# The causal triangle in PSUM behind each unit's maximum, and the forget gates' logarithm on other engines

## The chip, the cores and the metric

The kernel runs on one core of a Trainium2 chip. The metric is the device time of one execution in microseconds (us), as the median of several runs. Beside the runs there is one execution taken with the hardware profiler; its rows give the start and the duration of every instruction on every engine. TensorE (PE) multiplies matrices, and its weight loads (PEld) overlap with its matmuls. VectorE (DVE), ScalarE (ACT) and GpSimd (POOL) do the elementwise work, and SyncE (SP) issues most of the transfers. SBUF is the large on-chip memory; PSUM is the small one into which PE writes, in banks of 512 fp32 numbers per partition. PE, ACT and DVE touch PSUM in this kernel, POOL does not.

## The reference

One layer over 1024 tokens of width 1024. The input is normalised, scaled and shifted, and projected at once to the queries, keys, values and gates of two groups of eight heads of width 64, and to eight forget gates. Cut to what the change touches:

```python
log_f = log_sigmoid(ff + b_f)                    # (seq, 8 heads)
f_cum = cumsum(log_f, axis=seq)

# forgetting attention (FoX), for a block of 128 queries against all keys so far
s = q @ k.T * scale
s = s + (f_q[:, None] - f_k[None, :])
s = where(k_pos <= q_pos, s, -inf)               # the causal triangle
p = softmax(s)
out = p @ v

# stick-breaking attention, in the other eight heads
z = q @ k.T * scale
log_keep = where(k_pos < q_pos, log_sigmoid(-z), 0)
w = where(k_pos < q_pos, exp(log_sigmoid(z) + sum of the later log_keep), 0)
out = w @ v
```

The head outputs are multiplied by SiLU gates, projected, multiplied by a gate, added to the residual and normalised again. Since the softmax is taken over keys, the term `f_q` of a query drops out of it; the kernel only uses `-f_cum` of the keys.

## The kernel before, in words

All matrix products are taken with each operand split into a high and a low fp32r part, so that one product costs three matmuls (`L256` to `L258` for the projections `m`, `L311` to `L313` for the values, `L833` to `L835` for the output).

Attention is cut into 128 **units** (p, h, i): pair of heads p (0 to 3 are stick-breaking, 4 to 7 are FoX), head h in the pair, block of 128 queries i. A unit has 128 x (i+1)*128 scores `S` (`L411`, `L412`), all of them in one PSUM tile of two banks. A stick-breaking unit then runs two sigmoids on ACT (`kp` `L430`, `be` `L431`), a running product on DVE (`L436`, `L440`) that reads a tile `floor` in PSUM, and a multiplication on POOL (`L442`). A FoX unit runs, on DVE, one custom instruction that adds the forget row `fb` to the scores and takes the maximum (`a`, `nm`, `L418`), on ACT the exponential with its sum `l` (`L423`), on DVE the reciprocal of `l` (`L424`), and on POOL the scaling (`L425`). Two units later PE transposes the weights (`T`, `L459`), ACT and DVE copy them out as high part (`pt`, `L461`) and low part (`L462`), and after every second unit PE multiplies them with the values into a tile `pv` (`L474`): 4 to 16 matmuls, first those of the high parts, then those of the low parts. ACT and DVE evacuate `pv` (`L493`, `L494`).

**The forget gates.** The raw gates `fsb` come out of the value product of group 1 (`L323`). `forget_logs` makes log-sigmoid of them as min(x,0) - ln(1+exp(-|x|)): |x| on DVE (`L343`), exponential and logarithm on ACT (`L344`, `L345`), the rest on DVE (`L346`), and a scan over the blocks of 128 tokens on DVE (`L349`). Twelve steps later `forget_rows` sums over the tokens with two matmuls into `fcum` (`L360`, `L361`), copies the negative out on ACT (`L363`), transposes it on PE (`frow`, `L366`) and stores it to `f_dr` in HBM, from where `load_fb` reads a row of 1024 numbers for each head, on 128 partitions at once (`L375`, on ACT's queue).

**The triangle.** `att_causal` (`L396`) adds a 128 x 128 triangle of zeros and -1e30 to the diagonal block of `fb`, on DVE, before the unit that needs it. For i running downwards, the block that was masked for one unit is never read again by the later ones of that head.

**Order.** PE's order is written out by hand: for each unit the scores, a share of projection work from a list of fillers, `pv` of finished pairs, transposes, more fillers. The order of SP, DVE, ACT and POOL is that of a planner that simulates a timeline while the program is built and puts each instruction on its engine where it expects its inputs to be ready; `after(...)` pins an instruction behind another. Each engine runs its list strictly in that order.

**PSUM.** Eight banks: two for `acc`, two for `T`, two for `S`, one called `pv` and one called `fl`. In the first half `fl` holds `floor`; in the second half `pv_tile` alternates between `pv` and `fl`.

## Time and profile before

| | |
|---|---|
| median of 3 runs | 699.13 us (698.71 to 699.32) |
| profiled execution, its own time | 699.99 us |
| its span, first to last instruction | 698.2 us |
| granted clock of TensorE | 0.996 |
| PE busy | 676.0 us, 97% of the span |
| DVE, ACT, POOL busy | 483.7, 385.0, 410.6 us |
| stick-breaking units | about 93 to 357 us |
| FoX units | about 355 to 626 us |
| last matmul ends | 690.05 us |

A row of the timeline has: start, duration, engine, line and operation, output<-inputs, shapes, how many instructions were merged, and in square brackets the idle time of the engine before it with what ended it. A row of a list of waits has: who waited for whom, the microseconds in total, how often, and the longest. PE is busy nearly all the time, so what another engine does costs time only where PE stands and waits.

### The profile page before, as it was taken

Reading aid. Unit: us, or ns where it says so; the run is one execution under the profiler, and the core shown is the slowest. Engines: PE = TensorE matmul, PEld = TensorE weight load, DVE = VectorE, ACT = ScalarE, POOL = GpSimd, SP = SyncE. Lnnn points to the kernel's source line nnn. Section 1 sums busy time; section 2 is a strip of 40 time slices with the busy share of each in tenths; the row PEclk is TensorE's granted clock in tenths of the full one; section 3 lists DMA queues with packets and bytes.
Section 4 is the critical chain, followed back from the end, with each engine's and each line's share of the span. In section 5 each row is a group of like instructions: output and inputs, shape, how many; then the busy total and the mean of one; then the engine's idle time right before and its main releaser. Section 6 shows DMA issues by size and latency. Waiting matters only on the chain.

```text
span 698.2 us, 11781 instructions
## 1 busy us (share of the span) xinstructions
PE 676.0 (97%) x4033; PEld 589.0 (84%) x4033; DVE 483.7 (69%) x931; ACT 385.0 (55%) x866; POOL 410.6 (59%) x530
## 2 busy tenths in 40 slices
PE   7999989999999999999999999999999999999995
PEld 4789887888997888889988877889988889888884
DVE  5985678767657676767686684758576767784644
ACT  5667567856658576666664554645564666531000
POOL 4560487656437566556388897868483464665412
PEclk9999999999999999999999999999999999999998
DMA  8953451112102122112144554345241299143301
GB/s 313 415 215 128 113 176 53 28 39 49 42 9 69 40 53 55 38 46 61 29 134 145 174 164 155 112 116 164 95 143 51 58 283 364 56 162 113 119 31 60
DMA packets 44027, 81.59 MB, mean 117 GB/s; under 512 B 5120, under 2 KB 18880, under 8 KB 43072
## 3 DMA queue, kind: packets, MB, share of 16 engines
q1 hardware_dynamic: 42816, 76.65, 33.5%
q10 hardware_dynamic: 1152, 4.19, 2.0%
q8 instruction: 32, 0.52, 0.3%
q14 instruction: 27, 0.22, 0.1%
HBM read 60.34 MB, written 16.29 MB: 110 GB/s over the span
## 4 chain that ended last, share of the span: by engine, by line
PE 76%; DVE 7%; DMA 5%; POOL 4%; ACT 4%; issue 3%; SPq 0%; POOLq 0%; DVEq 0%; ACTq 0%
PE pv L474 9%; PE m L256 8%; PE m L257 8%; PE m L258 8%; PE T L459 8%; PE o L835 4%; PE o L833 4%; PE o L834 4%; PE S L412 4%; PE S L411 4%; PE v L311 3%; PE v L313 3%; PE v L312 3%; DMA wss<-in_w_ss_dram 1%; DMA raw<-in_w_qkg_dram 1%
## 5 line engine op out<-in xcount | busy, mean ns | idle before, releaser
L256 PE MATMUL m<-uh,whi 128*128 128x512 f32 x304 | 126.3, 415 | 0.5 <-DVE kl L244 0.5
L257 PE MATMUL m<-ul,whi 128*128 128x512 f32 x304 | 119.8, 394 | 0.0
L258 PE MATMUL m<-uh,wlo 128*128 128x512 f32 x304 | 119.6, 394 | 0.0
L462 DVE TENSOR_TENSOR pt<-T,pt 128x512 fp32r<-128x512 f32 (+2 forms) x192 | 100.6, 550 | 16.1 <-ACT pt L461 14.9
L442 POOL TENSOR_TENSOR be<-be,kp 128x127 f32<-128x127 f32 (+3 forms) x64 | 77.1, 1205 | 34.9 <-DVE kp L440 25.9
L461 ACT CAST pt<-T 128x512 fp32r<-128x512 f32 (+2 forms) x192 | 85.7, 480 | 17.2 <-PE T L459 13.6
L436 DVE TENSOR_TENSOR_SCAN kp<-kp,floor 128x512 f32<-128x512 f32 (+2 forms) x64 | 65.2, 1018 | 32.4 <-ACT kp L430 31.4
L474 PE MATMUL pv<-pt,v 128*128 128x256 f32 (+3 forms) x640 | 81.7, 272 | 3.8 <-DVE pt L462 3.8
L474 PEld LDWEIGHTS pv<-pt,v 128*128 128x128 f32 (+1 forms) x640 | 77.4, 163 | 9.0 <-DVE pt L462 4.7
L425 POOL TENSOR_SCALAR a<-a,l 128x1024 f32<-128x1024 f32 (+3 forms) x64 | 48.3, 755 | 43.8 <-DVE l L424 31.2
L423 ACT ACTIVATE a<-a,nm 128x1024 f32<-128x1024 f32 (+3 forms) x64 | 49.8, 778 | 40.5 <-DVE nm L418 40.1
L258 PEld LDWEIGHTS m<-uh,wlo 128*128 128x128 f32 x304 | 57.1, 188 | 13.5
L411 PE MATMUL S<-k,q 128*128 128x512 f32 (+5 forms) x192 | 66.6, 348 | 1.5 <-ACT be L431 0.8
L412 PE MATMUL S<-kl,qz 128*128 128x512 f32 (+5 forms) x192 | 65.5, 342 | 0.0
L256 PEld LDWEIGHTS m<-uh,whi 128*128 128x128 f32 x304 | 57.3, 188 | 9.2 <-DVE kl L244 0.9
L257 PEld LDWEIGHTS m<-ul,whi 128*128 128x128 f32 x304 | 57.4, 189 | 8.0
L495 POOL TENSOR_TENSOR ty<-ty,sg 64x256 f32<-64x256 f32 x64 | 47.7, 745 | 26.5 <-DVE ty L494 12.5
L418 DVE CUSTOM_DVE_ANT_0 a<-S,fb 128x1024 f32<-128x1024 f32 (+3 forms) x64 | 48.2, 754 | 15.9 <-PE S L412 7.8
L430 ACT ACTIVATE kp<-S 128x128 f32<-128x128 f32 (+3 forms) x64 | 41.7, 651 | 31.9 <-PE S L412 28.6
L311 PE MATMUL v<-whi_v,uh 128*128 128x256 f32 (+1 forms) x192 | 56.0, 292 | 0.7 <-DVE kl L244 0.7
L389 ACT CAST qz<-q 64x128 fp32r<-64x128 f32 x128 | 37.4, 295 | 31.3 <-PE S L412 30.0
L313 PE MATMUL v<-wlo_v,uh 128*128 128x256 f32 (+1 forms) x192 | 54.2, 282 | 0.0
(284 smaller groups left out, 1628.6 us busy)
## 6 DMA issues: line engine op xcount, KB each, us to landing
raw<-in_w_qkg_dram SPq DMA_DIRECT2D x38, 256.0 KB, 3.0
wss<-in_w_ss_dram SPq DMA_DIRECT2D x7, 1024.0 KB, 9.0
x<-in_x_dram SPq DMA_DIRECT2D x8, 512.0 KB, 7.1
k<-k SPq DMA_DIRECT2D x32, 128.0 KB, 2.3
wg<-in_w_gate_dram SPq DMA_DIRECT2D x8, 512.0 KB, 5.0
raw_o<-in_w_out_dram SPq DMA_DIRECT2D x16, 256.0 KB, 2.7
fb<-f_dr ACTq DMA_DIRECT2D x8, 512.0 KB, 4.3
wo_dr<-whi_o SPq DMA_DIRECT2D x16, 256.0 KB, 2.4
```

What stands on the lines that cost most here:

```text
L256: nc.tensor.matmul(acc, hi[:, c], u_hi[kt][:, s], start=(kt == 0), stop=False)
L257: nc.tensor.matmul(acc, hi[:, c], u_lo[kt][:, s], start=False, stop=False)
L258: nc.tensor.matmul(acc, lo[:, c], u_hi[kt][:, s], start=False, stop=(kt == NB - 1))
L311: nc.tensor.matmul(acc[:, :n], u_hi[kt][:, ts_], hi[:, s], start=(kt == 0), stop=False)
L313: nc.tensor.matmul(acc[:, :n], u_hi[kt][:, ts_], lo[:, s], start=False, stop=(kt == NB - 1))
L411: nc.tensor.matmul(S[:, s, :w], qst[p][h][:, qs], kst[p][h][:, ks], start=True, stop=False)
L412: nc.tensor.matmul(S[:, s, :w], z, klo[p][:, ks], start=False, stop=True)
L436: nc.vector.tensor_tensor_scan(rv, rv, floor[0][:, 512 - n:][:, ::-1], initial=0.0, op0=ALU.mult, op1=ALU.max)
L442: nc.gpsimd.tensor_tensor(be[:, :ke - 1], be[:, :ke - 1], kp[:, 1:ke], op=ALU.mult)
L461: nc.scalar.copy(hi[:, :n, qo:qo + P], t3)
L462: nc.vector.tensor_tensor(lo[:, :n, qo:qo + P], t3, hi.bitcast(F32)[:, :n, qo:qo + P], op=ALU.subtract)
L474: nc.tensor.matmul(acc[:m, q0:256], vt[p][:, kb, h * P:h * P + m], pt[:, kb % 4, q0:], start=start, stop=stop)
```

## The change

Three things change.

1. **Log-sigmoid** is made as min(x,0) + ln(sigmoid(|x|)): |x|, sigmoid and logarithm on ACT, the minimum and the sum on POOL. The scan over blocks leaves this step.
2. **The sums of the gates.** Two matmuls write to two parts of one PSUM tile: the totals of all blocks (ones x `flf`, 65 columns) and the sums within a block. The scan over blocks runs on DVE from PSUM, in `forget_rows`; DVE instead of ACT then combines and negates the two.
3. **The triangle** is copied once to PSUM by ACT (`ps_causal`), into the bank `fl`, after the last stick-breaking unit's scores are issued. `pv_tile` no longer alternates: all of `pv` goes through one bank. Each add of the triangle is pinned behind the maximum of the preceding unit; the very first one, which still reads the triangle from SBUF, is pinned behind the last running product of the stick-breaking units.

```diff
     def forget_logs():
         ff = fsb.rearrange("p h t -> p (h t)")
         ab = cp.tile([P, 64], F32, tag="fab", name="fab")
         lf = flf[:, 1:]
-        nc.vector.scalar_tensor_tensor(ab, ff, -1.0, ff, op0=ALU.mult, op1=ALU.max)
-        nc.scalar.activation(ab, ab, AF.Exp, scale=-1.0)
-        nc.scalar.activation(ab, ab, AF.Ln, bias=1.0)
-        nc.vector.scalar_tensor_tensor(lf, ff, 0.0, ab, op0=ALU.min, op1=ALU.subtract)
-        pre = ff
-        nc.vector.tensor_tensor_scan(pre, flf[:, 0:64], later.rearrange("p h t -> p (h t)"), initial=0.0,
-                                     op0=ALU.add, op1=ALU.mult)
-        return lf, pre
+        nc.scalar.activation(ab, ff, AF.Abs)
+        nc.scalar.activation(ab, ab, AF.Sigmoid)
+        nc.scalar.activation(ab, ab, AF.Ln)
+        nc.gpsimd.tensor_scalar(ff, ff, 0.0, 1.0, op0=ALU.min, op1=ALU.mult)
+        nc.gpsimd.tensor_tensor(lf, ff, ab, op=ALU.add)
+        return lf
 ...
-        fp = t_tile("fcum")[:, :64]
-        nc.tensor.matmul(fp, tri, lf, start=True, stop=False)
-        nc.tensor.matmul(fp, ones.to_broadcast([P, P]), pre, start=False, stop=True)
+        fp = t_tile("fcum")
+        nc.tensor.matmul(fp[:, 64:129], ones.to_broadcast([P, P]), flf, start=True, stop=True)
+        nc.tensor.matmul(fp[:, :64], tri, lf, start=True, stop=True)
+        pre = fsb.rearrange("p h t -> p (h t)")
+        nc.vector.tensor_tensor_scan(pre, fp[:, 64:128], later.rearrange("p h t -> p (h t)"), initial=0.0,
+                                     op0=ALU.add, op1=ALU.mult)
         fc = cp.tile([P, 64], F32, tag="fab", name="fc")
-        nc.scalar.activation(fc, fp, AF.Copy, scale=-1.0)
+        nc.vector.scalar_tensor_tensor(fc, fp[:, :64], -1.0, pre, op0=ALU.mult, op1=ALU.subtract)
 ...
-            nc.vector.tensor_tensor(f[:, dg], f[:, dg], causal, op=ALU.add)
+            nc.vector.tensor_tensor(f[:, dg], f[:, dg], ps_causal[0][:, :P] if ps_causal else causal, op=ALU.add)
 ...
-            nc.vector.tensor_tensor_reduce(out=v3(a), in0=S[:, :ns, :w], in1=v3(f),
+            rows = nc.vector.tensor_tensor_reduce(out=v3(a), in0=S[:, :ns, :w], in1=v3(f),
                                            op0=ALU.add, op1=ALU.min, scale=-1.0, scalar=BIG,
                                            accum_out=nm)
             if following:
-                att_causal(following)
+                with after(rows):
+                    att_causal(following)
 ...
+            with after(scan):                      # scan: the unit's last running product
+                att_causal(following)
 ...
-        acc = pv_tile(f"pv_{p}_{h}_{j}", p >= 4 and j % 2 == 1)
+        acc = pv_tile(f"pv_{p}_{h}_{j}")
 ...
             if k == 16 * 4 - 1:
                 load_fb(0)
                 load_fb(1)
-                att_causal(units[k + 1])
 ...
+            if k == 16 * 4 - 1:
+                ps_causal.append(ps.tile([P, 512], F32, tag="fl", bufs=1, name="ps_causal"))
+                nc.scalar.copy(ps_causal[0][:, :P], causal)
```

What this does to the engines' lists is seen in two places. The orders of PE and SP stay as they were, but for the two matmuls of `fcum` changing places; the lines up to 342 keep their numbers, later ones move by up to five.

First, DVE's list around the forget gates (`fsb` are the gates, `kp_1_1_7` and `kp_2_0_0` the running products of two successive units, `pt1` the low parts of transposed weights, `T` the transposes). Before:

```order
L462 TENSOR_TENSOR pt1_1_1_2_1_2443<-T_1_1_4_1_2444,pt0_1_1_2_1_2442 128x128
L343 SCALAR_TENSOR_TENSOR fab_2460<-fsb_129 128x64
L436 SCALAR_TENSOR_TENSOR kp_1_1_7_2471<-kp_1_1_7_2471,floor_863 128x512
L440 SCALAR_TENSOR_TENSOR kp_1_1_7_2471<-kp_1_1_7_2471,floor_863 128x512
L346 SCALAR_TENSOR_TENSOR flf_130<-fsb_129,fab_2460 128x64
L349 SCALAR_TENSOR_TENSOR fsb_129<-flf_130,later_132 128x64
L462 TENSOR_TENSOR pt1_1_1_2_0_2434<-T_1_1_5_0_2494,pt0_1_1_2_0_2433 128x4x128
L462 TENSOR_TENSOR pt1_1_1_2_1_2443<-T_1_1_5_1_2501,pt0_1_1_2_1_2442 128x2x128
```

After the change:

```order
L465 TENSOR_TENSOR pt1_1_1_2_1_2443<-T_1_1_4_1_2444,pt0_1_1_2_1_2442 128x128
L437 SCALAR_TENSOR_TENSOR kp_1_1_7_2471<-kp_1_1_7_2471,floor_863 128x512
L441 SCALAR_TENSOR_TENSOR kp_1_1_7_2471<-kp_1_1_7_2471,floor_863 128x512
L465 TENSOR_TENSOR pt1_1_1_2_0_2434<-T_1_1_5_0_2494,pt0_1_1_2_0_2433 128x4x128
L465 TENSOR_TENSOR pt1_1_1_2_1_2443<-T_1_1_5_1_2501,pt0_1_1_2_1_2442 128x2x128
```

Three instructions have left the stretch, and the low parts of unit (1,1,5) now follow the running product directly. The scan and the negation stand further down the list, behind the running product of unit (2,0,4).

Second, DVE's list where FoX goes over from one pair of heads to the next (`fb_2` and `fb_3` are the forget rows of the two heads of pair 5, `fb_1` that of the second head of pair 4, `a` and `nm` the weights and the maximum of a unit; unit (5,0,7) with `fb_2` follows unit (4,1,0)). Before:

```order
L418 ISA a_4_1_0_5038,nm_4_1_0_5039<-S_4_1_0_5035,fb_1_4121 128x128
L418 ISA nm_4_1_0_5039 128x1
L424 RECIPROCAL l_4_1_0_5040<-l_4_1_0_5040 128x1
L396 TENSOR_TENSOR fb_3_5047<-fb_3_5047,causal_71 128x128
L250 SCALAR_TENSOR_TENSOR sg_5_4885<-sg_5_4885,m_5_2_0_4995 128x512
L462 TENSOR_TENSOR pt1_4_1_1_0_5021<-T_4_1_2_0_5072,pt0_4_1_1_0_5020 128x3x128
L418 ISA a_5_0_7_5095,nm_5_0_7_5096<-S_5_0_7_5090,fb_2_4620 128x1024
```

After the change:

```order
L418 ISA a_4_1_0_5041,nm_4_1_0_5042<-S_4_1_0_5038,fb_1_4122 128x128
L418 ISA nm_4_1_0_5042 128x1
L396 TENSOR_TENSOR fb_2_4623<-fb_2_4623,ps_causal_4138 128x128
L425 RECIPROCAL l_4_1_0_5043<-l_4_1_0_5043 128x1
L250 SCALAR_TENSOR_TENSOR sg_5_4888<-sg_5_4888,m_5_2_0_4998 128x512
L465 TENSOR_TENSOR pt1_4_1_1_0_5024<-T_4_1_2_0_5075,pt0_4_1_1_0_5023 128x3x128
L418 ISA a_5_0_7_5098,nm_5_0_7_5099<-S_5_0_7_5093,fb_2_4623 128x1024
```

The first add to `fb_3`, which only unit (5,1,7) needs, stood eight units ahead of that one, right behind the unit after which the load of `fb_3` is issued. Now the place holds the add to `fb_2` for the very next unit, with the triangle from PSUM; `fb_2` was loaded eight units earlier. The first adds to `fb_2` and to `fb_4` to `fb_7` move in the same way.

More of the change, by code (lines that the diff above doesn't have):

```diff
@@ L342, in forget_logs, with forget_rows @@
         lf = flf[:, 1:]
-        nc.vector.scalar_tensor_tensor(ab, ff, -1.0, ff, op0=ALU.mult, op1=ALU.max)
-        nc.scalar.activation(ab, ab, AF.Exp, scale=-1.0)
-        nc.scalar.activation(ab, ab, AF.Ln, bias=1.0)
-        nc.vector.scalar_tensor_tensor(lf, ff, 0.0, ab, op0=ALU.min, op1=ALU.subtract)
-        pre = ff
-        nc.vector.tensor_tensor_scan(pre, flf[:, 0:64], later.rearrange("p h t -> p (h t)"), initial=0.0,
-                                     op0=ALU.add, op1=ALU.mult)
-        return lf, pre
-    def forget_rows(lf, pre):
+        nc.scalar.activation(ab, ff, AF.Abs)
[4 more added lines that the diff above has]
+        return lf
+    def forget_rows(lf):
         scratch = att_tile("fscratch")
@@ L378, in tile_hybrid_layer @@
     st_w, st_pt = {}, {}
-    floor = []
+    floor, ps_causal = [], []
     zq = {}
@@ L435, in att_scores @@
             rv = kp[:, ke - n:ke][:, ::-1]
-            nc.vector.tensor_tensor_scan(rv, rv, floor[0][:, 512 - n:][:, ::-1], initial=0.0,
-                                         op0=ALU.mult, op1=ALU.max)
+            scan = nc.vector.tensor_tensor_scan(rv, rv, floor[0][:, 512 - n:][:, ::-1], initial=0.0,
+                                                op0=ALU.mult, op1=ALU.max)
             if ke > n:
                 rv = kp[:, :ke - n][:, ::-1]
-                nc.vector.tensor_tensor_scan(rv, rv, floor[0][:, 0:1].to_broadcast([P, ke - n]),
-                                             initial=kp[:, ke - n:ke - n + 1], op0=ALU.mult, op1=ALU.max)
+                scan = nc.vector.tensor_tensor_scan(rv, rv, floor[0][:, 0:1].to_broadcast([P, ke - n]),
+                                                    initial=kp[:, ke - n:ke - n + 1], op0=ALU.mult, op1=ALU.max)
+            with after(scan):
+                att_causal(following)
             nc.gpsimd.tensor_tensor(be[:, :ke - 1], be[:, :ke - 1], kp[:, 1:ke], op=ALU.mult)
@@ L774, in gen_forget @@
             yield
-        yield from forget_rows(*logs)
+        yield from forget_rows(logs)
     wo = {}
```

## The prediction

> **What bounds the kernel now.** The page's busy times and the list of waits of TensorE come first, since a change elsewhere can only win back what TensorE stands still (columns of a wait: total us, times, longest):
>
> ```profile
> PE 676.0 (97%) x4033; PEld 589.0 (84%) x4033; DVE 483.7 (69%) x931; ACT 385.0 (55%) x866; POOL 410.6 (59%) x530
> ...
> PE pv L474 <- DVE pt L462: 3.8, 5, 1.6
> PE sc_all L163 <- DVE sc L160: 3.3, 1, 3.3
> ...
> 690.09 0.42 DVE L848 SCALAR_TENSOR_TENSOR r<-xr,o 128x256 f32<-128x256 f32 x1 [1.94 <-PE o L835]
> ```
>
> The span is 698.2 us, so PE is idle for 22.2 us of it. 3.3 of them come before the first matmul, and 8.1 behind the last one, whose result DVE takes at 690.09; the change touches neither. So some 11 us are left to be won between, and nearly half of them are in these rows of PE's timeline:
>
> ```profile
> 220.85 0.98 PE L474 MATMUL pv<-pt,v 128*64 128x256 f32 x7 [1.64 <-DVE pt L462]
> 410.19 1.06 PE L459 MATMUL T<-ident,a 128*128 128x128 f32 x7 [0.24 <-DVE pt L462]
> 411.44 0.50 PE L411 MATMUL S<-k,q 128*128 128x512 f32 x1 [0.19 <-DVE nm L418]
> 414.79 1.22 PE L474 MATMUL pv<-pt,v 128*64 128x256 f32 x9 [0.41 <-DVE pt L462]
> 433.69 0.75 PE L474 MATMUL pv<-pt,v 128*64 128x256 f32 x5 [1.21 <-DVE pt L462]
> 469.00 0.74 PE L474 MATMUL pv<-pt,v 128*64 128x256 f32 x5 [0.15 <-DVE pt L462]
> 541.98 0.44 PE L411 MATMUL S<-k,q 128*128 128x384 f32 x1 [0.50 <-DVE nm L418]
> ```
>
> All of them wait for DVE. The reader is to see that each has a cause in what the change edits. A further point is how to size them: a matmul of 512 columns is shown with 0.40 us, yet the next one starts 0.23 us later.
>
> ```profile
> 217.82 0.40 PE L256 MATMUL m<-uh,whi 128*128 128x512 f32 x1
> 218.05 0.40 PE L257 MATMUL m<-ul,whi 128*128 128x512 f32 x1
> ```
>
> So a matmul's shown end lies some 0.16 us behind the moment at which the next could have followed, and every stop of PE is 0.16 us longer than its bracket.
>
> **The forget gates' logarithm.** DVE, ACT and POOL around 217 us, before the change:
>
> ```profile
> 214.54 1.28 ACT L344 ACT_TABLE_LOAD   x1
> 215.83 0.26 ACT L344 ACTIVATE fab<-fab 128x64 f32<-128x64 f32 x1
> 216.11 1.28 ACT L345 ACT_TABLE_LOAD   x1
> 217.57 0.84 ACT L461 CAST pt<-T 128x512 fp32r<-128x512 f32 x2
> 218.43 1.28 ACT L430 ACT_TABLE_LOAD   x1
> ...
> 217.69 1.23 DVE L346 SCALAR_TENSOR_TENSOR flf<-fsb,fab 128x64 f32<-128x64 f32 x1 [0.94 <-ACT fab L345]
> 218.95 1.26 DVE L349 TENSOR_TENSOR_SCAN fsb<-flf,later 128x64 f32<-128x64 f32 x1
> 220.13 0.99 DVE L462 TENSOR_TENSOR pt<-T,pt 128x512 fp32r<-128x512 f32 x2
> ...
> 218.79 2.51 POOL L126 TENSOR_TENSOR wlo<-raw,whi 128x512 fp32r<-128x512 f32 x2
> ```
>
> DVE waits 0.94 us for the logarithm, and two instructions of 64 elements then take 2.5 us, while POOL runs back to back. The low parts that PE wants (`L462`) start only at 220.13. The change takes these DVE instructions away and, by the order, puts the low parts right behind the running product. On ACT the sigmoid needs no load of its own, as the stick-breaking units use it; the order has one load fewer in this place. ACT's part is then |x|, sigmoid, load, logarithm: 214.5 + 0.26 + 0.26 + 1.28 + 0.26 = 216.6 (0.26 as in the `fab` row, for each of the three), so the high parts follow at 216.6 instead of 217.57, and the low parts end near 216.6 + 0.6 + 1.1 = 218.3. PE wants them at 220.85 - 1.64 = 219.2. The stop goes: 1.64 + 0.16 = 1.80 us, with 0.9 us to spare.
>
> [...]
>
> The two instructions on POOL come to its list between `L125`, `L442` and `L126`. Nothing of that size is in the trace: each lies between nothing and half of the 2.51 us that two `L126` of eight times the elements take. Fixed costs apart, an eighth of 1.25 is 0.16, so I take 0.3. POOL is then 0.6 us later at 221, where the product `be` of the next unit waits for it; its transposes come two units later. Nothing on PE, then.
>
> **The sums.** The scan and the negation now stand between the matmuls of `fcum` and the transpose `frow`, on DVE:
>
> ```profile
> 236.92 0.39 PE L361 MATMUL fcum<-fsb,ones 128*128 128x64 f32 x2
> 237.63 0.48 DVE L440 TENSOR_TENSOR_SCAN kp<-kp,floor 128x128 f32<-128x128 f32 x1
> 239.34 0.27 PE L366 MATMUL frow<-ident,fc 128*64 128x128 f32 x1
> ```
>
> By the order they follow `L440`, which ends at 238.11. A scan of 128 elements takes 0.48 here, so 64 take at most that; with 0.3 us for each of the two (my estimate, from that scan), `fc` is ready near 238.7, 0.6 us ahead of the transpose. Nothing, then; if the scan takes the 1.26 us of the old `L349`, `fc` is ready at 239.7 and PE stops for some 0.5 us. I take 0 and keep both ends for the range. The evacuation `L494` that they push back by 0.6 us has no reader before the next `pv`.
>
> **The triangle.** Its group, one of DVE's whose reading side is PSUM, and what DVE waits for there:
>
> ```profile
> L396 DVE TENSOR_TENSOR fb<-fb,causal 128x128 f32<-128x128 f32 x64 | 39.1, 612 | 12.7 <-DMA fb<-f_dr 11.5
> L320 DVE TENSOR_TENSOR v<-v,v 128x128 fp32r<-128x128 f32 x34 | 9.6, 282 | 6.2 <-ACT v L319 5.8
> ```
>
> The same shape takes 612 ns on the mean with both inputs in SBUF and 282 with one in PSUM. So 64 x 0.33 = 21 us of DVE's time go, and with them 11.5 us of standing for the transfer of `fb`. What counts is where PE was stopped by it:
>
> ```profile
> 404.77 4.15 DVE L396 TENSOR_TENSOR fb<-fb,causal 128x128 f32<-128x128 f32 x1
> 431.70 0.87 DVE L396 TENSOR_TENSOR fb<-fb,causal 128x128 f32<-128x128 f32 x1 [3.75 <-DMA fb<-f_dr]
> 467.03 0.85 DVE L396 TENSOR_TENSOR fb<-fb,causal 128x128 f32<-128x128 f32 x1 [2.78 <-DMA fb<-f_dr]
> 535.47 0.90 DVE L396 TENSOR_TENSOR fb<-fb,causal 128x128 f32<-128x128 f32 x1 [1.15 <-DMA fb<-f_dr]
> ...
> 407.49 1.29 POOL L126 TENSOR_TENSOR wlo_o<-raw_o,whi_o 128x512 fp32r<-128x512 f32 x1
> 408.75 0.66 POOL L125 TENSOR_SCALAR whi_o<-raw_o 128x512 fp32r<-128x512 f32 x1
> ```
>
> At 404.77 the add lasts until POOL, busy without a gap, goes from one instruction to the next at 408.75; the stops of 0.24 and 0.19 follow. At 431.70, 467.03 and 535.47 the add was put right behind the load of `fb`, and the stops of 1.21, 0.15 and, by way of a late maximum, exponential and evacuation, 0.50 follow. In the new order each add stands behind the maximum of the preceding unit, eight units after its load (the 35 us from 431.70 to 467.03). So these five go: 0.24 + 0.19 + 1.21 + 0.15 + 0.50 + 5 x 0.16 = 3.09 us. The 0.41 at 414.79 has its low parts behind the next unit's maximum in the list; it may shrink, and I count nothing for it.
>
> [...]
>
> **What takes something back.** First, the add to `fb_0` still reads SBUF and stands between the last running product and the low parts that PE needs:
>
> ```profile
> 356.73 2.00 POOL L442 TENSOR_TENSOR be<-be,kp 128x1023 f32<-128x1023 f32 x1 [0.44 <-DVE kp L440]
> ...
> 355.37 1.28 DVE L440 TENSOR_TENSOR_SCAN kp<-kp,floor 128x512 f32<-128x512 f32 x1
> 356.74 1.01 DVE L462 TENSOR_TENSOR pt<-T,pt 128x512 fp32r<-128x512 f32 x2
> ...
> 357.47 1.48 PE L474 MATMUL pv<-pt,v 128*128 128x256 f32 x12
> ```
>
> It costs 0.3 us if it gets in ahead of POOL's product, and up to the 4.15 us seen above if not. ACT's copy of the triangle, some 0.3 us, waits for the same running product. I take 0.5 for both. Second, `pv` has one bank instead of two. A tight place of the last pair shows the time for its evacuation:
>
> ```profile
> 588.62 1.94 PE L474 MATMUL pv<-pt,v 128*128 128x256 f32 x16
> 591.38 0.43 DVE L494 TENSOR_TENSOR ty<-pv,ty 64x256 f32<-64x256 f32 x1 [0.22 <-ACT ty L493]
> 595.45 1.48 PE L474 MATMUL pv<-pt,v 128*128 128x256 f32 x12
> ```
>
> The bank is free at 591.81, the next product comes at 595.45: 3.6 us to spare. Nothing.
>
> **The sum.** -1.80 - 3.09 + 0.5 = -4.4 us. Against the profiled execution this is a span of 693.8; what lies around the span (699.99 - 698.2 = 1.8) stays. That execution is 0.9 us above the median, so from 699.13 I forecast 694.7.
>
> **Rivals.**
> Partial: the logarithm on ACT still comes late, for instance because ACT reaches |x| later than now, and the stop at 220.85 stays. For it speaks that the high parts follow the logarithm on ACT; against it the 0.9 us to spare. 694.7 + 1.8 = 696.5.
> Nothing to see: the add at the hand-over is kept out by POOL as at 404.77 and stops PE for about 4 us, of which 0.5 is in the sum: 694.7 + 3.6 = 698.3. For it speaks that POOL has 2.00 and more us of work ready at that moment; against it that POOL waits for the same running product and DVE's add is next in line.
> Slower: the single bank of `pv`. From the end of one product (590.56) to the next are 4.9 us; if copy and add come later than that, PE waits for DVE at `L474`. FoX has 32 such products; at 5.3 us each would cost 0.4 if all were as tight as this one: 694.7 + 13 = 708. Against it: the evacuation above takes 1.3 us from the end of the product, and the changed order leaves it where it was.
> That the change doesn't do what it says would be seen in the two loads of `L344` and `L345` both standing; the order speaks against it.
>
> **How the numbers follow.** The forecast has a chance of 0.78, the partial rival 0.07, nothing to see 0.10, slower 0.05. A measurement of this kernel tells some 0.2%, 1.4 us, from no change. Faster: 0.78 + 0.07 - 0.01 for a forecast that shrinks below 1.4 = 0.84; same 0.11; slower 0.05. The upper end of the range holds the partial case and goes to 698.0 for the unknown prices (hand-over, `frow`). The lower end: the stop at 414.79 goes too (0.57), the hand-over costs nothing (0.5), and stops shorter than 0.16 us, which have no bracket, give another 0.6: 693.0.
>
> **What would show it.** Right: the bracket of 1.64 at `pv` near 219 is gone; the add's mean is near 0.28 us with no wait for `fb`; PE's list of waits has no more than 1 us left for `pt` and `nm` after 350 us; PE's busy time is unchanged. Wrong: a wait of `pv` for `ty` (`L494` of before), a stop at `frow`, an add of several us near 356, or as many us of PE idle with other names in the brackets.

## The result, and the profile after

The changed kernel takes 694.4 us (median of 6 runs, 693.96 to 695.54), against 699.16 us for the kernel before (6 runs, 698.71 to 699.74): a ratio of 0.9934, with a 95% interval of 0.9923 to 0.9945. The forecast was 694.7 (693.0 to 698.0). The profiled execution of the changed kernel took 694.61 us, with a span of 692.6 and a granted clock of 0.996, the same as before; so nothing of the gain is a faster clock. Two runs of the batches below, at granted clocks of 0.85 and 0.75, took 743.96 and 832.57 us; ratios and spreads leave them out.

The page's busy times of the kernel after, and then its list of waits of TensorE (us in total, times, longest):

```profile
PE 674.5 (97%) x4033; PEld 589.2 (85%) x4033; DVE 462.3 (67%) x930; ACT 384.3 (55%) x866; POOL 410.1 (59%) x532
```

```profile
PE sc_all L163 <- DVE sc L160: 3.0, 1, 3.0
...
PE T L462 <- DVE pt L465: 0.9, 1, 0.9
...
PE pv L477 <- DVE pt L465: 0.4, 1, 0.4
...
PE S L411 <- DVE nm L418: 0.2, 1, 0.2
```

`pv` waited for `pt` five times and 3.8 us in all; now it is once, 0.4, at 119.14 among the first units, where nothing was changed. Of the seven stops that the prediction listed, one bracket is left in the timeline of PE after 200 us:

```profile
536.32 0.44 PE L411 MATMUL S<-k,q 128*128 128x384 f32 x1 [0.21 <-DVE nm L418]
```

Idle time of PE falls from 698.2 - 676.0 = 22.2 us to 692.6 - 674.5 = 18.1. The last result is taken from PE 5.68 us earlier (690.09 before), and from there to the end nothing has changed:

```profile
684.41 0.42 DVE L851 SCALAR_TENSOR_TENSOR r<-xr,o 128x256 f32<-128x256 f32 x1 [1.94 <-PE o L838]
```

Where the time went can be had more exactly than from brackets. Each matmul of the scores is found in both timelines, and the difference of its two starts is followed along the span: it moves only where one kernel stood and the other did not. The steps of this difference:

| place, in the time of before | what the prediction took off | what the step measures |
|---|---|---|
| 221, `pv` | 1.80 | 1.85 |
| 356, hand-over | +0.5 (a loss) | 0.15 off |
| 410 and 411 | 0.24 + 0.19 + 2 x 0.16 = 0.75 | 1.00 |
| 415 | 0 (0.57 if the stop went) | 0.65 |
| 434 | 1.37 | 1.41 |
| 469 | 0.31 | 0.35 |
| 524, not in the list | 0 | 0.16 |
| 542 | 0.66 | 0.29 |
| sum | 4.4 | 5.9 |

The stop at 524 had a bracket of 0.21 us, and PE waited for POOL there. It too fits an add that was held, the one in this row of the kernel before: the reciprocal behind it on DVE came late, and POOL stood 0.32 us for that. Of the kernels below only the whole change without PSUM, whose add there takes 1.42 us again, has this stop again.

```profile
521.07 1.42 DVE L396 TENSOR_TENSOR fb<-fb,causal 128x128 f32<-128x128 f32 x1
```

The two profiled executions differ by 699.99 - 694.61 = 5.4 us. Of the 5.9, 0.2 are missing because the units of after start that much later. Another 0.3 are lost outside the span: a run's time is 1.7 to 1.8 us longer than its span for the kernel before and 2.0 to 2.1 for the kernel after. The medians differ by 4.8: the execution of before lies 0.8 above its median, that of after 0.2 above.

Three places show how the stops went. Around 217 us, ACT, POOL, DVE and PE of the kernel after:

```profile
215.30 1.28 ACT L345 ACT_TABLE_LOAD   x1
216.59 0.26 ACT L345 ACTIVATE fab<-fab 128x64 f32<-128x64 f32 x1
216.75 0.84 ACT L464 CAST pt<-T 128x512 fp32r<-128x512 f32 x2
217.35 1.02 DVE L465 TENSOR_TENSOR pt<-T,pt 128x512 fp32r<-128x512 f32 x2 [1.19 <-ACT pt L464]
216.52 0.45 POOL L346 TENSOR_SCALAR fsb<-fsb 128x64 f32<-128x64 f32 x1
221.40 0.31 POOL L347 TENSOR_TENSOR flf<-fsb,fab 128x64 f32<-128x64 f32 x1
...
218.71 1.46 PE L477 MATMUL pv<-pt,v 128*128 128x256 f32 x12
```

One table load is left ahead of the logarithm, the low parts end at 218.37, and PE runs its twelve matmuls of `pv` without a stop. The sum on POOL comes only at 221.40, and nobody waits for it.

The rows of the sums, from the same timeline:

```profile
235.97 0.48 DVE L441 TENSOR_TENSOR_SCAN kp<-kp,floor 128x128 f32<-128x128 f32 x1
236.37 0.27 DVE L360 TENSOR_TENSOR_SCAN fsb<-fcum,later 128x64 f32<-128x64 f32 x1
236.67 0.22 DVE L363 SCALAR_TENSOR_TENSOR fc<-fcum,fsb 128x64 f32<-128x64 f32 x1
237.68 0.27 PE L366 MATMUL frow<-ident,fc 128*64 128x128 f32 x1
```

`fc` is ready at 236.89, 0.8 us ahead of the transpose. And the triangle, in DVE's groups of the kernel after:

```profile
L396 DVE TENSOR_TENSOR fb<-fb,ps_causal 128x128 f32<-128x128 f32 x63 | 17.9, 283 | 1.3
```

The mean is 283 ns where it was 612, and of the 11.5 us of standing for the transfer of `fb` nothing is left.

### The profile page after: what moved, and what is told of

It is laid out like the page before. It is cut to its first block, busy times and chain, and to the rows that moved or that the text cites. A ratio compares the mean times of both kernels' runs of the same rounds, so it can differ in the third digit from the quotient of the medians.

```text
span 692.6 us, 11784 instructions
## 1 busy us (share of the span) xinstructions
PE 674.5 (97%) x4033; PEld 589.2 (85%) x4033; DVE 462.3 (67%) x930; ACT 384.3 (55%) x866; POOL 410.1 (59%) x532
## 4 chain that ended last, share of the span: by engine, by line
PE 86%; DVE 5%; DMA 3%; ACT 3%; POOL 2%; issue 1%; SPq 0%; POOLq 0%; DVEq 0%; ACTq 0%
PE m L256 10%; PE m L257 10%; PE m L258 10%; PE pv L477 10%; PE T L462 9%; PE S L412 5%; PE S L411 5%; PE o L838 4%; PE o L836 4%; PE o L837 4%; PE v L311 4%; PE v L313 4%; PE v L312 4%; DMA wss<-in_w_ss_dram 1%; DMA x<-in_x_dram 1%
```

## The experiments

**The theory** was the prediction's: every stop that goes was DVE coming late with `pt` or `nm`, at 221 us through two short instructions and a late logarithm, after 400 us through adds that either stood for the transfer of `fb` or were held by POOL, that is, lasted until POOL went from one instruction to another; the parts add up. **The rivals**: one part does it all; the pins alone suffice; the pair of table loads (1.28 us each) is the cause at 221; the single bank of `pv` takes something back. Each ratio is against runs of the kernel before on the same chip; from a ratio follow the microseconds given with it, which differ by some tenths from the difference of the two medians.

### The two halves, apart

The kernel before with only `forget_logs` and `forget_rows` of the change:

```diff
-        nc.scalar.activation(ab, ab, AF.Exp, scale=-1.0)
-        nc.scalar.activation(ab, ab, AF.Ln, bias=1.0)
...
+        nc.scalar.activation(ab, ab, AF.Sigmoid)
+        nc.scalar.activation(ab, ab, AF.Ln)
+        nc.gpsimd.tensor_scalar(ff, ff, 0.0, 1.0, op0=ALU.min, op1=ALU.mult)
+        nc.gpsimd.tensor_tensor(lf, ff, ab, op=ALU.add)
```

> The kernel before with the forget gates' logarithm and sums of the change alone. My theory (only what TensorE stands still counts): the stop of 1.64 us at the pv product near 220 us goes and nothing else, so 1.8 us faster than before, and no bracket at frow. The rival (what counts is the time taken off the loaded engines, spread over the whole span): DVE loses 3.4 us here and 21 us by the triangle, so logs alone bring a seventh of the 4.8 us, 0.7 us.

Measured: 698.16 us against 699.15, ratio 0.998 (0.9972 to 0.9989), that is 1.4 us, between the 1.8 of the theory and the 0.7 of the rival that counts engine time. The steps decide for the theory: the one at 221 measures 1.85 us, and a run's time minus its span grows from 1.74 to 2.06 us, which takes 0.3 of it back. Of the later stops in the prediction's list only the 0.24 at 410 is missing; the others stand, as in this row of its PE timeline:

```profile
431.64 0.75 PE L474 MATMUL pv<-pt,v 128*64 128x256 f32 x5 [1.33 <-DVE pt L462]
```

The counterpart, the kernel before with the triangle in PSUM, the pins and one bank of `pv`, but the old logarithm:

```diff
-            nc.vector.tensor_tensor(f[:, dg], f[:, dg], causal, op=ALU.add)
+            nc.vector.tensor_tensor(f[:, dg], f[:, dg], ps_causal[0][:, :P] if ps_causal else causal, op=ALU.add)
...
+                with after(rows):
+                    att_causal(following)
```

> The kernel before with the triangle in PSUM, the pins and the one pv bank, but the old logarithm. My theory: the stop of 1.64 us near 220 stays, the stops at 410, 411, 433, 469 and 542 go or shrink, and the one at 415 too: 3 to 3.8 us faster than before. The rival of engine time: six sevenths of the 4.8 us, 4.1 us faster. The two theories are told apart by the trace: by mine the matmuls up to 400 us start at the same times as before, within 0.4 us.

Measured: 695.8 us against 699.15, ratio 0.9956 (0.9944 to 0.9968), 3.1 us. In its timeline the steps after 340 us are those of the whole change, one by one (4.0 us in sum), while the old stop stands:

```profile
221.27 0.98 PE L477 MATMUL pv<-pt,v 128*64 128x256 f32 x7 [1.64 <-DVE pt L465]
```

The two ratios multiply to 0.9936; the whole change, run again beside other kernels, has 0.9933 (below). So the halves add up, as far as these intervals tell.

### Pins without PSUM

Each add behind the preceding unit's maximum, as in the change, but the triangle stays in SBUF and `pv` keeps two banks:

```diff
-                att_causal(following)
+                with after(rows):
+                    att_causal(following)
```

> The kernel before with the pins alone: the triangle stays in SBUF, pv keeps its two banks. My theory: no wait for the transfer of fb is left, the stops of 1.21, 0.15 and 0.50 us go (2.3 us with what their brackets hide), but the add still takes 612 ns on the mean and some add is held for several us by POOL, wherever one falls, with a stop of some 0.5 to 1 us like that at 410: 1.5 to 2.3 us faster. The rival, that being held by POOL is the whole cost and the pins change nothing: no difference from before.

Measured: 697.35 us against 699.15, ratio 0.9976 (0.9968 to 0.9985), 1.7 us. In its groups the standing for `fb` is gone, but the add is nearly as long as before, 572 ns against 612:

```profile
L396 DVE TENSOR_TENSOR fb<-fb,causal 128x128 f32<-128x128 f32 x64 | 36.6, 572 | 1.2
```

And its timeline, POOL and DVE first, then what PE still stands for:

```profile
405.01 0.61 POOL L125 TENSOR_SCALAR whi_o<-raw_o 128x512 fp32r<-128x512 f32 x1
405.53 3.75 DVE L396 TENSOR_TENSOR fb<-fb,causal 128x128 f32<-128x128 f32 x1
405.59 1.28 POOL L123 TENSOR_TENSOR raw_o<-raw_o,gate 128x512 f32<-128x512 f32 x1
406.86 1.01 POOL L426 TENSOR_SCALAR a<-a,l 128x896 f32<-128x896 f32 x1
407.84 1.29 POOL L126 TENSOR_TENSOR wlo_o<-raw_o,whi_o 128x512 fp32r<-128x512 f32 x1
409.10 0.65 POOL L125 TENSOR_SCALAR whi_o<-raw_o 128x512 fp32r<-128x512 f32 x1
...
411.79 0.50 PE L411 MATMUL S<-k,q 128*128 128x512 f32 x1 [0.19 <-DVE nm L418]
415.14 1.22 PE L477 MATMUL pv<-pt,v 128*64 128x256 f32 x9 [0.41 <-DVE pt L465]
```

The add comes out only after POOL has gone from its product `L126` to the next instruction at 409.10, as at 404.77 in the kernel before. So the pins take the stops at 434 and 469 and a part of that at 542 (steps of 1.42, 0.35 and 0.30, the same as with the whole change), and the hold by POOL keeps most of those at 410 to 415: 0.4 us of 1.6 go. With the triangle in PSUM the same add of the kernel after runs within a POOL instruction of the same kind:

```profile
402.80 1.28 POOL L123 TENSOR_TENSOR raw_o<-raw_o,gate 128x512 f32<-128x512 f32 x1
402.94 0.29 DVE L396 TENSOR_TENSOR fb<-fb,ps_causal 128x128 f32<-128x128 f32 x1
```

So beside the same work of POOL the add takes 3.75 us with both inputs in SBUF and 0.29 with one of them in PSUM. What in the chip makes the difference no run shows.

The whole change without PSUM, so the new logarithm and the pins, is the same cut from the other side:

```diff
-            nc.vector.tensor_tensor(f[:, dg], f[:, dg], ps_causal[0][:, :P] if ps_causal else causal, op=ALU.add)
+            nc.vector.tensor_tensor(f[:, dg], f[:, dg], causal, op=ALU.add)
...
-        acc = pv_tile(f"pv_{p}_{h}_{j}")
+        acc = pv_tile(f"pv_{p}_{h}_{j}", p >= 4 and j % 2 == 1)
```

> The change but for PSUM: new logarithm and pins, the triangle stays in SBUF and pv keeps two banks. My theory: the sum of the two parts, 1.8 for the logarithm and 1.5 to 2.3 for the pins, 3.3 to 4.1 us faster than before and so 0.7 to 1.5 us slower than the whole change, because adds are again held by POOL. The rival (all adds that matter were those behind the load): as fast as the whole change.

Measured: 695.94 us against 698.94, ratio 0.9958 (0.9944 to 0.9972), 2.9 us. Its add is held again at the same place, and two of the stops behind it stand, 0.19 at `S` and this one:

```profile
403.12 3.83 DVE L396 TENSOR_TENSOR fb<-fb,causal 128x128 f32<-128x128 f32 x1
...
412.81 1.22 PE L477 MATMUL pv<-pt,v 128*64 128x256 f32 x9 [0.41 <-DVE pt L465]
```

So PSUM itself, on top of the pins, is worth the rest: 0.0025 of the time or 1.7 us with the new logarithm, from ratios of two batches, and 0.0020 or 1.4 us without it, from kernels of one batch (triangle_only against pin_only, medians 1.55 apart). By the steps at 410 to 415 it is 1.2 to 1.3 us in these two traces.

### PSUM without the pins behind the loads

As the second kernel, but the first adds to `fb_2` to `fb_7` go back right behind their loads, where they stand for the transfer:

```diff
             if following:
-                with after(rows):
-                    att_causal(following)
+                if not (following[2] == NB - 1 and 9 <= 2 * following[0] + following[1] < 16 and following[:2] not in ((4, 1),)):
+                    with after(rows):
+                        att_causal(following)
...
                 load_fb(2 * (p - 4) + h + 2)
+                q = 2 * p + h + 2
+                att_causal((q // 2, q % 2, NB - 1))
```

> The triangle's part of the change, but the first add to each of fb_2 to fb_7 is put back right behind the load of its row, as before. My theory: the adds take 0.28 us each and none is held by POOL, but DVE stands for the transfer of fb again (about 11 us in all), so the stops at 433, 469 and 542 come back and only those at 410 to 415 go: 1 to 1.6 us faster than before, 2 to 2.5 us slower than the triangle's part alone. The rival of POOL alone: as fast as the triangle's part alone.

Measured: 697.6 us (696.06 to 699.66, 12 runs) against 699.15, ratio 0.998 (0.997 to 0.9991). Its groups of DVE show the standing, 11.0 us of it, as before; and yet the `pv` at the place of the old stop of 1.21 has no bracket:

```profile
L396 DVE TENSOR_TENSOR fb<-fb,ps_causal 128x128 f32<-128x128 f32 x63 | 17.8, 284 | 12.1 <-DMA fb<-f_dr 11.0
```

```profile
430.07 0.29 DVE L396 TENSOR_TENSOR fb<-fb,ps_causal 128x128 f32<-128x128 f32 x1 [3.18 <-DMA fb<-f_dr]
...
430.97 1.26 PE L478 MATMUL pv<-pt,v 128*128 128x256 f32 x8
```

DVE stood for 3.18 us here, where it stood for 3.75 in the kernel before; the add behind it then took 0.29 instead of 0.87. The low parts are in time to within 0.27 us, by which these eight matmuls are longer than the 0.99 that they take elsewhere. In this execution the step at 434 is 1.15 of the 1.42 us, with most of the standing still there. The median, however, is 1.8 us above the kernel that has the pins as well, whose five runs went from 695.55 to 696.44. Profile and times disagreed, so the kernel was run a second time:

> The triangle's part with the first adds behind their loads, once more: its times went from 696.06 to 699.66 us, while one profile showed DVE standing 3.2 us for a row without a stop of TensorE. My theory: how long the load of a row takes differs between executions, and from some 3.5 us of standing on TensorE stops; this profile may show other stops near 433, 469 and 540, and the median stays 1 to 2.5 us slower than the whole triangle part at 695.8. The rival (standing for the load costs nothing once POOL holds no add): the same 695.8.

Measured: 697.62 us (695.83 to 699.07, 12 runs), ratio 0.9977 (0.9967 to 0.9987): the same time. And its profile shows again standing without a stop:

```profile
429.33 0.29 DVE L396 TENSOR_TENSOR fb<-fb,ps_causal 128x128 f32<-128x128 f32 x1 [2.87 <-POOL raw_o L123]
...
464.33 0.29 DVE L396 TENSOR_TENSOR fb<-fb,ps_causal 128x128 f32<-128x128 f32 x1 [3.00 <-DMA fb<-f_dr]
```

Here `pv` takes 0.99 again; so 0.3 us less of standing was worth 0.27 us of PE. (The first bracket is put down to POOL, but the row itself landed only at 429.23, 0.1 us before the add, as the rows of the kernel before land 0.09 us before the adds that stand for them.) That is a stop that varies with the arrival of the row: once the slack of DVE, 3.20 us there, is used up, each later us is a us of PE. The table further down shows this over seven traces. But the two executions that were profiled took 697.19 and 696.27, both below their median, and no execution with the longer times has a trace. That the 1.8 us are late rows is argued, not shown, and the longest standings in any trace, 3.85 us at 434 and 3.16 at 469, would by my estimate from that table lose only 1.1 us at both places together. It stays open.

### The single bank of pv

The kernel before with `pv` in one bank and nothing else:

```diff
-        acc = pv_tile(f"pv_{p}_{h}_{j}", p >= 4 and j % 2 == 1)
+        acc = pv_tile(f"pv_{p}_{h}_{j}")
```

> The kernel before with all pv products in one PSUM bank and nothing else. My theory: a bank is free 3 us or more ahead of the next product, so no wait of pv for its evacuation and no difference from before, within 0.5 us. The rival (the single bank holds TensorE up): some 0.4 us at each of 32 products, up to 13 us slower.

Measured: 698.39 us against 698.94, ratio 0.9998 (0.9988 to 1.0007). No `pv` waits for `ty`. The stops at 434, 469 and 542 stand as before (1.06, 0.16 and 0.50 us) and of those at 410 to 415 only the last (0.35), which has to do with the add and not with the bank: it was held for 3.07 us here, not 4.15. In the kernel after, the tightest place leaves 2.71 us between the evacuation of one product (end at 557.60) and the start of the next (560.31). Within the interval the bank costs nothing.

### What makes the stop at 221

Only the sigmoid in place of the exponential, so one table load of 1.28 us less, and |x| on ACT; the sum and the scan stay on DVE ahead of the low parts, and the sums of the gates are those of before:

```diff
-        nc.vector.scalar_tensor_tensor(ab, ff, -1.0, ff, op0=ALU.mult, op1=ALU.max)
-        nc.scalar.activation(ab, ab, AF.Exp, scale=-1.0)
-        nc.scalar.activation(ab, ab, AF.Ln, bias=1.0)
-        nc.vector.scalar_tensor_tensor(lf, ff, 0.0, ab, op0=ALU.min, op1=ALU.subtract)
+        nc.scalar.activation(ab, ff, AF.Abs)
+        nc.scalar.activation(ab, ab, AF.Sigmoid)
+        nc.scalar.activation(ab, ab, AF.Ln)
+        nc.vector.scalar_tensor_tensor(lf, ff, 0.0, ab, op0=ALU.min, op1=ALU.add)
```

> The logarithm by |x|, sigmoid and ln on ACT, with one table load less, but its sum and the scan stay on DVE in front of the low parts. My theory (DVE's two short instructions are held while POOL runs its long ones, and the low parts stand behind them): the sum is still held until POOL's product ends near 218.9 and the scan behind it, so the stop near 220 stays at 1.3 to 1.7 us and the time is as before, within 0.4 us. The rival (the table load on ACT is the cause): the stop goes, 1.8 us faster.

Only the work off DVE, so the exponential and both table loads stay (shown against `forget_logs` of the changed kernel; `forget_rows` is that of the change):

```diff
-        nc.scalar.activation(ab, ab, AF.Sigmoid)
-        nc.scalar.activation(ab, ab, AF.Ln)
+        nc.scalar.activation(ab, ab, AF.Exp, scale=-1.0)
+        nc.scalar.activation(ab, ab, AF.Ln, bias=1.0)
...
-        nc.gpsimd.tensor_tensor(lf, ff, ab, op=ALU.add)
+        nc.gpsimd.tensor_tensor(lf, ff, ab, op=ALU.subtract)
```

> The logarithm with exponential and ln(1+x) and both table loads as before, |x| on ACT, but the minimum, the sum and the scan off DVE's list in front of the low parts, as in the change. My theory: ACT frees itself at 217.9, the low parts follow the high parts and end near 219.6, so PE stops for 0.4 us or less: 1.3 to 1.8 us faster than before. The rival (the table load): the stop stays, no difference from before.

Measured: 698.17 us, ratio 0.9993 (0.9984 to 1.0002), for the sigmoid alone; 697.77, ratio 0.9989 (0.998 to 0.9998), for the work off DVE alone. The traces are plain, with steps at 221 of 0.47 and 1.65 us and, for the first, this row:

```profile
220.47 0.98 PE L474 MATMUL pv<-pt,v 128*64 128x256 f32 x7 [1.15 <-DVE pt L462]
```

The times are not: the two intervals overlap almost wholly, on a kernel whose single runs spread over 2.5 us, and the second falls short of the 1.3 to 1.8 us that were expected of it. The kernels with the whole triangle change spread less, so the same two were made again as cuts of the whole change, with the change itself beside them:

> The whole change once more, as the measure for the other three of this set. Expected by all theories: 4.2 to 5.3 us faster than before.

> The whole change, but the sum and the scan of the gates back on DVE in front of the low parts; only the logarithm by sigmoid, with one table load less, stays on ACT. My theory (DVE's list and being held by POOL make the stop near 220): a stop of 1.1 to 1.3 us as in the same edit on the kernel before, so 1.2 to 1.5 us slower than the whole change. The rival (the table load): as fast as the whole change.

> The whole change, but the logarithm by exponential and ln(1+x), with both table loads of before. My theory: the stop near 220 is at most 0.2 us, so within 0.3 us of the whole change. The rival (the table load): the stop is back, 1.8 us slower than the whole change.

Measured, against 699.02: the whole change 694.45 (694.16 to 694.53, 5 runs), ratio 0.9933 (0.9921 to 0.9945); with sum and scan back on DVE 695.51 (695.03 to 695.56), ratio 0.9947 (0.9936 to 0.9959); with the exponential back 694.92 (694.67 to 695.27), ratio 0.9942 (0.9929 to 0.9955). All runs of the two cuts lie above all of the whole change; between themselves they overlap by a little (695.03 against 695.27). By the medians, then, the sum and the scan on DVE cost 1.06 us and the second table load 0.47; the old logarithm whole, the triangle alone in an earlier batch, had 695.8, which is 1.35 above. But with the sum and the scan on DVE a run's time is again only 1.73 us longer than its span, where it is 2.05 with them off DVE. Within the span they cost 1.4 us (medians of 693.8 against 692.4), and the steps say the same: 0.50 at 221 where the whole change has 1.85. With the exponential back the step is 1.64, so the load is 0.21 us there; where the rest of its 0.47 lies isn't shown. The timeline of the kernel with sum and scan on DVE shows how:

```profile
215.90 2.00 POOL L445 TENSOR_TENSOR be<-be,kp 128x1023 f32<-128x1023 f32 x1
217.86 2.51 POOL L126 TENSOR_TENSOR wlo<-raw,whi 128x512 fp32r<-128x512 f32 x2
216.26 1.72 DVE L346 SCALAR_TENSOR_TENSOR flf<-fsb,fab 128x64 f32<-128x64 f32 x1 [0.73 <-ACT fab L345]
218.02 1.27 DVE L349 TENSOR_TENSOR_SCAN fsb<-flf,later 128x64 f32<-128x64 f32 x1
219.21 0.99 DVE L465 TENSOR_TENSOR pt<-T,pt 128x512 fp32r<-128x512 f32 x2
219.92 0.98 PE L477 MATMUL pv<-pt,v 128*64 128x256 f32 x7 [1.14 <-DVE pt L465]
```

The sum starts at 216.26, 1.4 us earlier than in the kernel before, since the load is gone. It gains little by that: it ends at 217.98, just behind the place where POOL goes from one product to the next (217.86), and the scan ends at 219.29, just behind the middle of POOL's two `L126` (219.1). Two instructions of 64 elements take 3 us, because each lasts until POOL changes instruction. The next low parts are 0.99 us behind that, and PE stands for 1.14. With the exponential back, and sum and scan on POOL and from PSUM, there is no bracket:

```profile
218.74 1.02 DVE L465 TENSOR_TENSOR pt<-T,pt 128x512 fp32r<-128x512 f32 x2 [2.48 <-ACT pt L464]
218.81 1.66 PE L477 MATMUL pv<-pt,v 128*128 128x256 f32 x12
```

The low parts end at 219.76, 1.4 us later than in the kernel after, and the twelve matmuls take 1.66 instead of 1.46: 0.2 us, hidden in a duration. So the stop at 221 was mainly DVE's two short instructions held by POOL, and the load the smaller part. None of these kernels beats the changed one.

## Why the prediction was right, and where its sizes were off

**The logarithm** (1.80) was right: 1.85 by the step, the same when done alone, the low parts at 218.37 where 218.3 was forecast. The step named two causes, the wait of 0.94 us for the logarithm and 2.5 us of two instructions; the cuts show that the second carries most of it: taken away alone it gives a step of 1.65, the load alone one of 0.47, and the two together no more than 1.85. The two instructions on POOL take 0.45 and 0.31 where 0.3 was taken for each; no wait of PE follows from it. What failed is a term of the sum: that what lies around the span stays. It grew by 0.3 us in every kernel that has the minimum and the sum on POOL (2.0 to 2.1 us) and in no other (1.7 to 1.8). Which of the edits that go with them does it isn't shown.

**The sums** (0, with 0.5 as the bad end) were right: the scan takes 0.27, `fc` is ready 0.8 us ahead of the transpose, 0.6 were forecast.

**The triangle** (3.09) was right in sum and partly right by accident. The five stops that it counted gave 1.00 + 1.41 + 0.35 + 0.29 = 3.05. Against 0.75 for the stops of 410 and 411 the step is 1.00. The stop at 415, counted as nothing because its low parts stand behind the next maximum, went entirely, 0.65: it was the tail of the same hold, for triangle_only has nearly the same step (0.61), while the pins alone leave its bracket of 0.41. The stop at 542 was forecast to go whole and went by 0.29 of 0.66: 0.21 of its bracket stays in every kernel with the pins, so this part has another cause, which the runs don't show. And the stops at 434 and 469 were put down to standing for the row. That was a part of the cause: pinned away from the row they go, but with PSUM alone they go too, or nearly, in the two executions that were traced, where the row came somewhat earlier and the add took 0.29 us.

The traces of all runs together say how much. What PE lost at a place is had from the starts of the matmuls, against the kernel after, from 385 to 425 us and from 425 to 445; "pinned" is an add that comes long after its row:

| kernel | add at 405, us | lost at 410 to 415 | standing + add at 432 | lost at 434 |
|---|---|---|---|---|
| before | 4.15 | 1.61 | 3.75 + 0.87 = 4.62 | 1.42 |
| new logarithm and sums (logs_only) | 3.90 | 1.37 | 3.34 + 1.41 = 4.75 | 1.55 |
| the change without PSUM (logs_pin) | 3.83 | 1.28 | pinned | 0 |
| pins alone (pin_only) | 3.75 | 1.22 | pinned | 0 |
| gate work off DVE (off_dve_only) | 3.64 | 1.09 | 3.55 + 1.00 = 4.55 | 1.35 |
| one bank of `pv` (one_bank) | 3.07 | 0.53 | 3.85 + 0.62 = 4.47 | 1.27 |
| sigmoid (sigmoid_only) | 2.65 | 0.11 | 3.46 + 1.36 = 4.82 | 1.61 |
| PSUM, adds behind loads (psum_early) | 0.29 | 0 | 3.18 + 0.29 = 3.47 | 0.27 |
| the same, second time | 0.29 | 0 | 2.87 + 0.29 = 3.16 | 0 |
| after | 0.29 | 0 | pinned | 0 |

Two of the adds, of one_bank and of sigmoid_only:

```profile
405.02 3.07 DVE L396 TENSOR_TENSOR fb<-fb,causal 128x128 f32<-128x128 f32 x1
```

```profile
404.45 2.65 DVE L396 TENSOR_TENSOR fb<-fb,causal 128x128 f32<-128x128 f32 x1
```

In the third column the loss is the length of the add less 2.54 us, to within 0.02, in all seven kernels whose triangle is in SBUF; in the last it is the standing and the add together less 3.20. (At 469 the same working gives 3.28.) So these are the amounts that DVE had in hand at the two places, and each us beyond them is a us of PE. At 434 the standing of the kernel before with an add of 0.29 us would still have lost 3.75 + 0.29 - 3.20 = 0.84 us (worked out, not run): standing made a bit over half of that stop and the hold the rest. The hold at 405 depends on where the add falls in POOL's work (it starts 0.10 us behind POOL's `L125` at 404.67 in the kernel before and lasts 4.15; with the pins alone it starts 0.52 us behind the same instruction and lasts 3.75), and that differs between the traces: that of the kernel before, from which the prediction read its stops, has the longest of the seven. So what PSUM buys there is 0.1 to 1.6 us, and that the sum was read from the trace with the most to win there was chance.

**The price of the hand-over** (+0.5, and up to 4.15) was too high: nothing was lost. The rows are these, of the kernel after:

```profile
353.25 1.30 POOL L126 TENSOR_TENSOR wlo_o<-raw_o,whi_o 128x512 fp32r<-128x512 f32 x1
353.61 1.09 DVE L396 TENSOR_TENSOR fb<-fb,causal 128x128 f32<-128x128 f32 x1
353.73 0.27 ACT L963 COPY ps_causal<-causal 128x128 f32<-128x128 f32 x1 [0.59 <-DVE kp L441]
354.83 1.01 DVE L465 TENSOR_TENSOR pt<-T,pt 128x512 fp32r<-128x512 f32 x2
355.64 1.47 PE L477 MATMUL pv<-pt,v 128*128 128x256 f32 x12
```

The add was indeed held, until POOL's `L126` ended at 354.55: 1.09 us, between the two bounds. But the low parts end at 355.84, and `pv` begins with the high parts at 355.64 and stands for nothing. The rival "nothing to see" needed the add to be held over several instructions of POOL; it was held over one.

**The single bank** (0) was right; the room at the tightest place is 2.71 us instead of the 3.6 that were read at one place of the last pair.

**Reading PSUM** was given no price of its own in the sum. The shortest adds, which show no hold, tell what it costs. The source lines of before and of after (shortest, median, longest, in ns):

```profile
L396 DVE TENSOR_TENSOR fb<-fb,causal x64: 271/352/4154, 350.8 to 618.1; 128x128 f32<-128x128 f32 x64
```

```profile
L396 DVE TENSOR_TENSOR fb<-fb,ps_causal x63: 269/286/290, 357.2 to 612.5; 128x128 f32<-128x128 f32 x63
```

269 ns from PSUM against 271 from SBUF at the shortest: the input in PSUM costs nothing that shows here, and what it buys is the narrow spread, 290 at the longest against 4154.

**The signs.** No bracket of 1.64 at `pv`, no wait for `fb`, 0.21 us left for `pt` and `nm` after 350 where up to 1 was allowed, no wait of `pv` for `ty`, none at `frow`: all as forecast. **"PE's busy time is unchanged"** alone was off by 1.5 us (676.0 to 674.5). The total is a poor measure: the second traced execution of the same kernel has 675.4, and the two differ in the first 100 us (93.0 against 94.0). Behind 100 us both are alike, 581.5 and 581.4 against 582.9 of the kernel before, so some 1.4 us did go. The prediction had a reason that fits: a matmul's shown end lies 0.16 us behind the moment at which the next could have followed, so the last matmul ahead of a stop shows 0.16 us of busy time that otherwise lies under its follower. Nine or so stops that go make 1.4 us. That is worked out, not measured by itself.

All in all -5.9 us by the steps instead of -4.4: 0.65 + 0.16 of stops that were not counted, 0.65 at the hand-over, and -0.37 for the one that half stayed make 1.1 of the 1.5; the rest is stops a little longer than bracket plus 0.16. From the 5.9, the later start of the units (0.2), the growth around the span (0.3) and the two executions' distances from their medians (0.8 - 0.2) lead to the 4.8 at the medians. That this lies so close to the sum of 4.4 is partly luck: more went than was counted, and 0.3 came back at a place that the sum took as fixed.

## What to carry to other kernels

Where TensorE is the bound, look for the small instructions of DVE that stand directly ahead of what TensorE wants: one of 64 elements with both inputs in SBUF lasted 1.2 to 1.7 us beside a busy POOL, one of 128 up to 4.15, and moving one of its inputs to PSUM, or its work to another engine, brought it to 0.2 to 0.45. An add that depends on a transfer is best put where its result is needed and not where the transfer is issued; both cures, made apart, may take away the same stop, so their gains must not be added before both have been run alone. Matmuls can hide a stop of some tenths of a us inside a merged duration (twelve took 1.66 instead of 1.46 us, eight 1.26 instead of 0.99), so compare starts of the same instruction in two traces, not only the brackets. And read a stop in more than one execution before you count on it: the same one measured 0.1 to 1.6 us here.

## What the runs showed of the hardware that was not expected

- **A held add lasts over several instructions of POOL.** In the kernel with the pins alone it started at 405.53; POOL changed instruction at 405.59, 406.86 and 407.84, and only behind the next change, at 409.10, did the add come out, at 409.28. The hold returns at the same place in all seven kernels with the triangle in SBUF (2.65 to 4.15 us). In the two rows above that have POOL's beside them, of the kernel before (end at 408.92) and of the pins alone, it ends just behind the change of POOL from `L126` to `L125` (408.75 and 409.10). Why at this change and not at an earlier one isn't shown.
- **The scan of 64 elements**: 1.26 us from SBUF beside POOL (1.27 in the kernel with sum and scan back on DVE), 0.27 from PSUM, where it ended at 236.64 while a product of POOL ran from 236.54 to 237.86.
- **The spread of the runs.** The changed kernel's five runs in the last batch lie within 0.37 us, the 17 of the kernel before beside them within 2.3. All kernels with pins and PSUM stay within 1.6 us, and in the same batches all whose adds stand for the row spread over 2.2 to 3.6, though with 10 to 29 runs against 5 or 6. The pins alone, with 11 runs, have 1.8. The load of the row that the add at 432 stands for took 4.72 us from issue to landing in the kernel before, whose eight loads of rows took 3.75 to 4.86; the add came 4.82 us behind the issue there, 4.92 in one_bank and 4.24 in psum_early. That its varying arrival makes the spread would fit, but no trace of a long execution was taken.
